# A decoder layer on one Trainium2 core: the forgetting heads' bias loaded as causal strips of the running sums, without the query's own sum

## The chip, the cores and the metric

The kernel runs on one core of a Trainium2 chip. It is one launch that computes a whole decoder layer. The time is device microseconds of that core. Five engines work side by side, each in the order of its own instruction stream: TensorE (PE; its weight loads are listed as PEld), VectorE (DVE), ScalarE (ACT), GpSimd (POOL) and SyncE (SP). Here SP does nothing but issue DMA transfers; they are numbered as work of its queue, SPq. An engine that meets an instruction whose operands are not there yet stands still, and everything behind that instruction in its stream stands still with it.

Times come from whole executions of the kernel (the median of several) and from one more execution that was recorded by the profiler, which has a time of its own.

## The reference: what is computed

One sequence of 512 positions with 1024 features goes through a half-step feed-forward block, a mixer, and a second half-step feed-forward block. The mixer projects the normalised input by one wide matrix to the queries, keys and values of two attention branches of 8 heads each, with gates, and merges the two. This case concerns branch A, the forgetting attention:

```python
def fox_attention(q, k, v, log_f):
    S = q.shape[1]
    cum = jnp.cumsum(log_f, axis=1).transpose(0, 2, 1)
    scale = HEAD_DIM ** -0.5
    for start in range(0, S, Q_BLOCK):                     # Q_BLOCK = 128
        end = start + Q_BLOCK
        logits = einsum('bqhd,bkhd->bhqk', q[:, start:end], k[:, :end]) * scale
        logits = logits + cum[:, :, start:end, None] - cum[:, :, None, :end]
        logits = where(kpos <= qpos, logits, NEG_INF)
        p = softmax(logits, axis=-1)
        outs.append(einsum('bhqk,bkhd->bqhd', p, v[:, :end]))
```

`log_f` is one number per head and position. Its running sum `cum` enters a logit twice: with the query's position t (plus) and with the key's position s (minus). Within one row of a softmax the query's term is the same for all keys. Branch B is a sparse attention: an indexer scores all keys, the top 128 of each query stay, and a bias by distance is added.

## The kernel before

**Tiling.** There are 16 heads in the kernel's loop (`for g in range(2 * H)`): heads 0 to 7 are the forgetting ones, 8 to 15 the sparse ones. Each head has four blocks of 128 queries, worked from the last to the first: step s = 0, 1, 2, 3 is block i = 3, 2, 1, 0. Block i sees n = 128 (i + 1) keys, so its tiles are 128 x 512, 384, 256 and 128.

**One block** is the function `softmax_block`, and goes through all engines:

- the bias of the block is made (`bias(i)`);
- TensorE multiplies queries and keys into one of two PSUM buffers (`stack_mm`, lines 928 and 929). The scores carry the opposite sign, so the softmax works with a minimum in place of a maximum;
- VectorE adds the bias and takes each row's minimum `mn` in one instruction (line 1238);
- ScalarE takes the exponential, with each row's sum `rs` (line 1240);
- VectorE inverts `rs` (line 1241), and POOL multiplies the row by it (line 1242), giving the probabilities `p`.

**Values.** One head later, `flip` transposes the probabilities (TensorE, line 1249). The first of a head's four transposed tiles takes a 128 x 128 piece of all four blocks, so it needs `p` of block 0, the last one made. ScalarE and VectorE split the transposed tile into a rounded part `ph` (1253) and a rest `pl` (1254), and `weigh` multiplies both by the values (lines 1259 and 1260). `head_out` adds up a head's output (POOL in line 1270 for the first heads, VectorE splits it in line 1274).

**What fills TensorE.** Between these small products the loop runs pieces of the large projections (`prod.run`), whose weights SP loads (line 143), ScalarE rounds (144) and VectorE splits (150). Beside the first forgetting head the top-k of the sparse branch still runs on VectorE (lines 1187 to 1192), and the key projections are normalised on POOL (`kn`, line 1002; `rh`, line 900).

**The bias of a forgetting head.** A late piece of the indexer's stage, `forget`, computes the running sums: `cum` holds them with positions on the partitions, `ncum` (line 1174, VectorE) is their negative, and a transposed copy goes to a DRAM array `cum_rows` of 8 rows of 512. For head g, `get_bias(g)` loads row g once, repeated on all 128 partitions (line 1306, one DMA of 256 KB into a tile `cb` of which there are two). For each block, `bias(i)` then takes a scratch tile and has POOL do

```python
G.tensor_scalar(b[:, :n], cb[:, :n], 1.0, ncum[:, i, g:g + 1], op0=OP.mult, op1=OP.add)   # line 1312
G.affine_select(out=b[:, i * P:n], in_=b[:, i * P:n], ..., fill=BIG, ...)                   # line 1313
```

The first adds the query's own sum to the key's, the second writes a large number over the keys behind the query in the last 128 columns. The row of head g + 1 is loaded at step 0 of head g. For the sparse heads the same function loads another bias, and POOL subtracts.

**What sets the order.** TensorE's order is that of the program text. The instructions of VectorE, ScalarE, POOL and SP are put in order by a scheduler before the kernel is built, from its own estimate of when each could run; the order is fixed from then on. A change of some instructions makes the scheduler lay out all four streams anew. A tile name with two buffers lets the second user of a buffer start when all readers of the first are done, and a whole tile is released at once.

## Time and profile before

| | before |
|---|---|
| median of 3 timed runs | 1047.29 us (1047.10 to 1047.31) |
| the profiled execution's own time | 1047.09 us |
| its span | 1045.4 us |
| mean granted TensorE clock | 0.999 |
| TensorE busy | 1033.6 us (99%) |
| VectorE busy | 852.9 us (82%) |
| ScalarE busy | 669.0 us (64%) |
| POOL busy | 259.3 us (25%) |

The span is the time from the first to the last recorded instruction; the execution's own time is 1.7 us longer. A busy share is an average over stages: POOL is busy for 25% of the span, but the page's row of 40 slices shows it at 8 to 9 tenths in one slice and at 1 tenth in many others. A gap is a stretch in which an engine has nothing running; the profile puts in brackets how long it was and which instruction's end ended it. Where line numbers are named without more, they are those of the kernel before; from the change on, those of the functions above lie two lower.

### The profile page before, as it was taken

To read this page: it belongs to the slowest core of one execution; us is meant where nothing else is said; L and a number is where in the kernel's file an instruction comes from. 1 tells how busy PE (TensorE), PEld (TensorE's weight loads), DVE (VectorE), ACT (ScalarE), POOL (GpSimd) and SP (SyncE) were. 2 spreads that over 40 slices of the span, in tenths; PEclk is the share of its full clock that TensorE was granted. 3 is DMA by queue.
4 is the path that set the end of the run, shared out by engine and by line. 5 is a ranking of instruction groups with operands and counts; after the bars stand their busy time and mean duration, and the time that the engine had idled before them with its cause. 6 is when DMAs were issued, how large, how long until landed. Compare 5 with 4: busy or idle time off the path is not lost.

```text
span 1045.4 us, 19485 instructions
## 1 busy us (share of the span) xinstructions
PE 1033.6 (99%) x7424; PEld 962.6 (92%) x7424; DVE 852.9 (82%) x1405; ACT 669.0 (64%) x1118; POOL 259.3 (25%) x324
## 2 busy tenths in 40 slices
PE   9999999999999999999999999999999999999998
PEld 8889999999999898989977788888889999999998
DVE  6897888897989689977778765854887888988887
ACT  6547765865777766567867665433735865775773
POOL 1100111120121024386977653000100210111111
PEclk9999999999999999999999999999999999999999
DMA  7444765666567358633324321532553666567554
GB/s 259 105 151 120 158 165 129 152 163 173 120 150 182 91 147 192 188 104 90 92 69 117 117 70 51 158 131 74 131 168 90 152 147 182 127 160 190 135 127 131
DMA packets 57341, 142.66 MB, mean 136 GB/s; under 512 B 6424, under 2 KB 15768, under 8 KB 57248
## 3 DMA queue, kind: packets, MB, share of 16 engines
q1 hardware_dynamic: 39600, 110.21, 34.7%
q0 software_dynamic: 17504, 30.94, 16.5%
q8 instruction: 58, 0.95, 0.4%
q10 hardware_dynamic: 144, 0.27, 0.1%
q14 instruction: 35, 0.29, 0.1%
HBM read 104.94 MB, written 3.42 MB: 104 GB/s over the span
## 4 chain that ended last, share of the span: by engine, by line
PE 86%; DVE 9%; POOL 2%; issue 2%; ACT 1%; DVEq 0%; POOLq 0%; ACTq 0%
PE pB L157 5%; PE pB L156 5%; PE pB L155 5%; PE pA L157 3%; PE pA L155 3%; PE pA L156 3%; PE ps_f L155 3%; PE ps_f L156 3%; PE ps_f L157 3%; PE dB L157 2%; PE dB L155 2%; PE dB L156 2%; DVE sc L1189 2%; DVE m L1187 2%; PE dA L156 2%
## 5 line engine op out<-in xcount | busy, mean ns | idle before, releaser
L123 ACT CAST wh<-s 128x1024 fp32r<-128x1024 f32 (+1 forms) x90 | 86.7, 963 | 66.1 <-PE pC L156 31.6
L130 DVE TENSOR_TENSOR wl<-s,wh 128x1024 fp32r<-128x1024 f32 (+1 forms) x90 | 100.2, 1113 | 20.0 <-ACT wh L123 20.0
L155 PE MATMUL ps_t<-wh,xh 128*128 128x256 f32 (+1 forms) x288 | 81.1, 282 | 0.0
L156 PE MATMUL ps_t<-wl,xh 128*128 128x256 f32 (+1 forms) x288 | 80.2, 279 | 0.0
L157 PE MATMUL ps_t<-wh,xl 128*128 128x256 f32 (+1 forms) x288 | 80.2, 279 | 0.0
L155 PE MATMUL pB<-tbh,wh 128*128 128x256 f32 x288 | 79.5, 276 | 0.0
L156 PE MATMUL pB<-tbl,wh 128*128 128x256 f32 x288 | 79.5, 276 | 0.0
L157 PE MATMUL pB<-tbh,wl 128*128 128x256 f32 x288 | 79.5, 276 | 0.0
L249 POOL DMA_DIRECT2D b<-gu x12 | 10.4, 864 | 220.4 <-DVE rb L449 89.4
L155 PE MATMUL ps_f<-xh,wh 128*128 128x512 f32 x152 | 60.8, 400 | 0.0
L157 PE MATMUL ps_f<-xh,wl 128*128 128x512 f32 x152 | 59.6, 392 | 0.0
L156 PE MATMUL ps_f<-xl,wh 128*128 128x512 f32 x152 | 59.6, 392 | 0.0
L1240 ACT ACTIVATE p<-p,mn 128x512 f32<-128x512 f32 (+1 forms) x64 | 36.0, 562 | 30.8 <-DVE mn L1238 30.5
L155 PEld LDWEIGHTS ps_t<-wh,xh 128*128 128x128 f32 x288 | 54.4, 189 | 0.4
L156 PEld LDWEIGHTS ps_t<-wl,xh 128*128 128x128 f32 x288 | 54.4, 189 | 0.4
L157 PEld LDWEIGHTS ps_t<-wh,xl 128*128 128x128 f32 x288 | 54.4, 189 | 0.0
L157 PEld LDWEIGHTS pB<-tbh,wl 128*128 128x128 f32 x288 | 54.1, 188 | 0.0
L155 PEld LDWEIGHTS pB<-tbh,wh 128*128 128x128 f32 x288 | 54.1, 188 | 0.0
L156 PEld LDWEIGHTS pB<-tbl,wh 128*128 128x128 f32 x288 | 54.1, 188 | 0.0
L575 POOL DMA_DIRECT2D gx<-e x20 | 23.9, 1241 | 119.6 <-ACT wh L123 99.9
L1242 POOL TENSOR_SCALAR p<-p,rs 128x512 f32<-128x512 f32 (+1 forms) x64 | 39.1, 614 | 57.8 <-DVE rs L1241 53.8
L1254 DVE TENSOR_TENSOR pl<-pt,ph 128x512 fp32r<-128x512 f32 (+1 forms) x64 | 31.0, 484 | 19.6 <-ACT ph L1253 19.4
(406 smaller groups left out, 4195.1 us busy)
## 6 DMA issues: line engine op xcount, KB each, us to landing
rf<-in_w_pair_dram SPq DMA_DIRECT2D x15, 512.0 KB, 4.1
rc<-in_w_pair_dram SPq DMA_DIRECT2D x12, 512.0 KB, 3.6
re<-in_w_pair_dram SPq DMA_DIRECT2D x12, 512.0 KB, 3.6
rd<-in_w_pair_dram SPq DMA_DIRECT2D x12, 512.0 KB, 3.9
rb<-in_w_pair_dram SPq DMA_DIRECT2D x12, 512.0 KB, 4.2
gx<-e POOLq DMA_DIRECT2D x22, 256.0 KB, 4.2
ra<-in_w_pair_dram SPq DMA_DIRECT2D x9, 512.0 KB, 3.5
rd<-in_w_halves_dram SPq DMA_DIRECT2D x12, 384.0 KB, 3.7
```

Source lines behind the costliest of these rows:

```text
L123: S.copy(wh[:, :f], raw[:, :f])
L130: V.tensor_sub(wl[:, :f], raw[:, :f], wh[:, :f].bitcast(F32))
L155: PE.matmul(out, lh, rh, start=start, stop=False, **more)
L156: PE.matmul(out, lh, rl, start=False, stop=False, **more)
L157: PE.matmul(out, ll, rh, start=False, stop=stop, **more)
L249: G.dma_start(l, src, accum_op=OP.add)
L575: G.dma_start(xa[:, d:d + 2, HT:], t["e"][part], accum_op=OP.add)
L1187: V.max(m8, sc[i])
L1189: V.match_replace(out=sc[i], in_to_replace=m8, in_values=sc[i], imm_value=-3e38)
L1240: S.activation(p, p, AF.Exp, bias=mn, scale=-1.0, accum_out=rs)
L1242: G.tensor_scalar(p, p, rs, 1.0, op0=OP.mult, op1=OP.mult)
L1254: V.tensor_sub(pl[:, sl], pt[:, sl], ph[:, sl].bitcast(F32))
```

## The change

A new function `causal_rows(g, i)` makes the bias of one block of a forgetting head. It loads the first n = 128 (i + 1) sums of row g, repeated on 128 partitions, as a strip of its own (line 1309 now), and writes the large number into the strip's last 128 columns in place (line 1310 now). VectorE's addition reads the strip itself. The addition of the query's own sum is left out, and with it `ncum`, its instruction, and the scratch tile of the bias. The softmax's result is the same without it.

So for each forgetting head there are four DMAs (of 128 x 512, 384, 256 and 128 numbers) in place of one, and four selects in place of four additions and four selects. The strips of blocks 3 and 2 take the two buffers that `cb` had. Those of blocks 1 and 0 lie side by side in one tile named `sg`, which an earlier stage used with 4 x (S_W - 128) columns and which is now 384 wide; there is one such tile. The strip of block 3 of head g + 1 is requested at step 0 of head g, that of block 2 at step 1, and those of blocks 1 and 0 at step 3. The sparse heads keep their bias as it was.

```diff
-        sg = at.tile([P, NT, S_W - 128], F32, name="sg")
+        sg = at.tile([P, 3 * P], F32, tag="sg", name="sg")[:, :NT * (S_W - 128)].rearrange("p (t c) -> p t c", t=NT)
...
-        cum = at.tile([P, NT, H], F32, name="cum")
-        ncum = at.tile([P, NT, H], F32, name="ncum")
...
+            cum = small.tile([P, NT, H], F32, tag="cr", bufs=1, name="cum")
             V.tensor_copy(cum, pc[:, :NT * H].rearrange("p (t h) -> p t h", t=NT))
-            V.tensor_scalar(ncum, cum, -1.0, None, op0=OP.mult)
...
+        def causal_rows(g, i):
+            if i:
+                strip = at.tile([P, T] if i > 1 else [P, 3 * P], F32, tag="cb" if i > 1 else "sg",
+                                bufs=2 if i > 1 else 1, name="cb")
+            else:
+                strip = strips[1][:, 2 * P:]
+            n = P * (i + 1)
+            nc.sync.dma_start(strip[:, :n], cum_rows[g:g + 1, :n].to_broadcast([P, n]))
+            G.affine_select(out=strip[:, i * P:n], in_=strip[:, i * P:n], compare_op=OP.is_ge, fill=BIG, base=0,
+                            pattern=[[-1, P]], channel_multiplier=1)
+            strips[i] = strip
+
+        strips = {}
+
+        def forget_bias(i):
+            return strips[i][:, :P * (i + 1)]
+
         def get_bias(g):
             cb = at.tile([P, T], F32, tag="cb", bufs=2, name="cb")
-            nc.sync.dma_start(cb, cum_rows[g:g + 1, :].to_broadcast([P, T]) if g < H else a["rel"][g - H])
+            nc.sync.dma_start(cb, a["rel"][g - H])
 
             def bias(i):
                 n = P * (i + 1)
                 b = tmp_tile("b")
-                if g < H:
-                    G.tensor_scalar(b[:, :n], cb[:, :n], 1.0, ncum[:, i, g:g + 1], op0=OP.mult, op1=OP.add)
-                    G.affine_select(out=b[:, i * P:n], in_=b[:, i * P:n], compare_op=OP.is_ge, fill=BIG, base=0,
-                                    pattern=[[-1, P]], channel_multiplier=1)
-                else:
-                    G.tensor_sub(b[:, :n], sc[i] if i else cpos, cb[:, T - n:T])
+                G.tensor_sub(b[:, :n], sc[i] if i else cpos, cb[:, T - n:T])
                 return b[:, :n]
             return bias
...
             if step == 24:
-                nb = get_bias(0)
+                for i in (3, 2, 1, 0):
+                    causal_rows(0, i)
...
-            q, k, bias = nq, nk, nb
+            q, k, bias = nq, nk, forget_bias if g < H else nb
...
                 if g + 1 < 2 * H:
-                    if s == 0:
+                    if g + 1 < H:
+                        for i in ((3,), (2,), (), (1, 0))[s]:
+                            causal_rows(g + 1, i)
+                    elif s == 0:
                         nb = get_bias(g + 1)
```

TensorE's stream is the same before and after. The other four are laid out anew. Three places show how.

POOL around head 0. Each row is one instruction; `x4` stands for four in a row. Rows with `p` normalise a block (512 wide is block 3, 128 wide block 0); the additions make the biases, the selects mask them. Before, from the last addition and the selects of head 0 on:

```order
L1312 TENSOR_SCALAR b<-cb,ncum 128x128
L1313 AFFINE_SELECT b<-b 128x128 x4
L1242 TENSOR_SCALAR p<-p,rs 128x512
L1312 TENSOR_SCALAR b<-cb,ncum 128x512
L1313 AFFINE_SELECT b<-b 128x128
L1242 TENSOR_SCALAR p<-p,rs 128x384
L1242 TENSOR_SCALAR p<-p,rs 128x256
L1242 TENSOR_SCALAR p<-p,rs 128x128
L1312 TENSOR_SCALAR b<-cb,ncum 128x384
```

The same place now:

```order
L1310 AFFINE_SELECT cb<-cb 128x128 x5
L1240 TENSOR_SCALAR p<-p,rs 128x512
L1310 AFFINE_SELECT cb<-cb 128x128
L1240 TENSOR_SCALAR p<-p,rs 128x384
L1240 TENSOR_SCALAR p<-p,rs 128x256
L1310 AFFINE_SELECT cb<-cb 128x128 x2
L1240 TENSOR_SCALAR p<-p,rs 128x128
L1310 AFFINE_SELECT cb<-cb 128x128
```

The additions are gone. The first five selects are those of head 0 and of block 3 of head 1; the next one is of block 2 of head 1, and the two that follow are those of blocks 1 and 0 of head 1. They stand ahead of the normalisation of head 0's block 0, where before no work for head 1's last two blocks stood. The same order of two selects ahead of block 0's normalisation is found in heads 3 and 5.

VectorE in head 2, around the addition for block 0 (`ps_qk,b 128x128`), the weight split of line 150 and the reciprocals. Before:

```order
L1238 ISA p,mn<-ps_qk,b 128x128
L1238 ISA mn 128x1
L1238 ISA p,mn<-ps_qk,b 128x512
L1238 ISA mn 128x1
L150 TENSOR_TENSOR wl<-rb,wh 128x1024
L1254 TENSOR_TENSOR pl<-pt,ph 128x128
L1241 RECIPROCAL rs<-rs 128x1 x2
```

Now:

```order
L1236 ISA p,mn<-ps_qk,cb 128x128
L1236 ISA mn 128x1
L896 TENSOR_SCALAR ss<-ss 128x8
L1239 RECIPROCAL rs<-rs 128x1
L1236 ISA p,mn<-ps_qk,cb 128x512
L1236 ISA mn 128x1
L150 TENSOR_TENSOR wl<-rb,wh 128x1024
L1252 TENSOR_TENSOR pl<-pt,ph 128x128
L1239 RECIPROCAL rs<-rs 128x1
```

One reciprocal (block 1's) now follows block 0's addition, with a small operation of the key normalisation ahead of it; the last one, block 0's, still follows the weight split.

SP, from the request of head 0's bias on, before:

```order
L1306 DMA cb<-cum_rows 128x512
L143 DMA rc<-in_w_fq_dram 128x1024
L1041 DMA kept<-gs 128x512
L1306 DMA cb<-cum_rows 128x512
L143 DMA ra<-in_w_fq_dram 128x1024
L1306 DMA cb<-cum_rows 128x512
L143 DMA rb<-in_w_fv_dram 128x1024
```

Now:

```order
L1309 DMA cb<-cum_rows 128x512
L1309 DMA cb<-cum_rows 128x384
L1039 DMA kept<-gs 128x512
L1309 DMA cb<-cum_rows 128x256
L1309 DMA cb<-cum_rows 128x128
L143 DMA rc<-in_w_fq_dram 128x1024
L143 DMA ra<-in_w_fq_dram 128x1024
L143 DMA rb<-in_w_fv_dram 128x1024
L1309 DMA cb<-cum_rows 128x512
```

The four strips of head 0 go out ahead of the next weight load, which before stood behind one row.

## The prediction

> **What bounds the kernel now.** I read the page first, then the busy time by stretches, then TensorE's own waits, then the timeline of each gap. From the page:

> ```profile
> span 1045.4 us, 19485 instructions
> PE 1033.6 (99%) x7424; PEld 962.6 (92%) x7424; DVE 852.9 (82%) x1405; ACT 669.0 (64%) x1118; POOL 259.3 (25%) x324
> ```

> TensorE is idle for only 1045.4 - 1033.6 = 11.8 us, and the change leaves TensorE's instructions and their order as they are. So only idle time can be won, and only where the forgetting heads run (432 to 537 us). The stretches of 40, 40 and 20 us there (columns: stretch, length, then busy PE, PEld, DVE, ACT, POOL, the granted clock, the DMA share and GB/s):

> ```profile
> 440.00:480.00 40.00, 36.20 (x291) 34.69 (x289) 31.73 (x83) 27.12 (x61) 31.89 (x44) 1.00 0.34 99
> 480.00:520.00 40.00, 39.60 (x312) 38.08 (x311) 30.81 (x78) 32.25 (x73) 29.12 (x46) 1.00 0.36 95
> 520.00:540.00 20.00, 18.92 (x100) 15.38 (x98) 15.79 (x35) 14.18 (x34) 16.26 (x23) 1.00 0.21 57
> ```

> TensorE is idle here for 3.80 + 0.40 + 1.08 = 5.28 us: the ceiling of any gain, although POOL is 73 to 81% busy. The clock is full and the DMA engines are two thirds empty. One row of TensorE's waits (whole span: total, count, longest), and the larger gaps in its timeline (in brackets, the idle time before the instruction):

> ```profile
> PE pt L1249 <- POOL p L1242: 3.1, 3, 1.5
> ...
> 440.94 0.33 PE L928 MATMUL ps_qk<-kh,st 128*128 128x128 f32 x1 [0.57 <-DVE mn L1238]
> ...
> 448.73 0.33 PE L1249 MATMUL pt<-ident,p 128*128 128x128 f32 x1 [1.48 <-POOL p L1242]
> ...
> 470.07 0.33 PE L928 MATMUL ps_qk<-kh,st 128*128 128x128 f32 x1 [0.34 <-DVE mn L1238]
> ...
> 477.67 0.33 PE L1249 MATMUL pt<-ident,p 128*128 128x128 f32 x1 [1.40 <-POOL p L1242]
> ...
> 524.40 0.39 PE L1260 MATMUL po<-pl,fv 128*128 128x256 f32 x1 [0.75 <-DVE pl L1254]
> ...
> 527.53 0.33 PE L1249 MATMUL pt<-ident,p 128*128 128x128 f32 x1 [0.22 <-POOL p L1242]
> ```

> 3.1 us of the 5.28 is one event in three heads: the flip of a head's probabilities (line 1249) waits for POOL's normalisation (line 1242) of the last block, block 0. I write p(0,0) for head 0, block 0, and DVE(0,0) for VectorE's addition of bias and scores there. The question for each head is when POOL reaches p(g,0).

> **Removed: 32 additions on POOL and one VectorE instruction.** POOL by group, 425 to 540 us (busy, mean ns, idle before):

> ```profile
> L1313 POOL TENSOR_SCALAR_AFFINE_SELECT b<-b 128x128 f32<-128x128 f32 x32 | 9.2, 306 | 0.3
> L1312 POOL TENSOR_SCALAR b<-cb,ncum 128x384 f32<-128x384 f32 x8 | 6.6, 831 | 0.0
> L1312 POOL TENSOR_SCALAR b<-cb,ncum 128x512 f32<-128x512 f32 x8 | 6.6, 821 | 10.1 <-DMA cb<-cum_rows 10.1
> ...
> L1312 POOL TENSOR_SCALAR b<-cb,ncum 128x256 f32<-128x256 f32 x8 | 5.7, 712 | 0.0
> ...
> L1312 POOL TENSOR_SCALAR b<-cb,ncum 128x128 f32<-128x128 f32 x8 | 3.0, 374 | 0.0
> ```

> POOL loses 6.6 + 6.6 + 5.7 + 3.0 = 21.9 us; the 32 selects (9.2 us) stay, now on the strips. Nearly all of it lies beside busy matmuls and is worth nothing. It counts in two places.

> *Head 2 (gaps 0.34 and 1.40 us).* Around its flip, and line 150's group over 334.9 to 690.9 us (least, median, most):

> ```profile
> 469.45 0.56 DVE L1238 CUSTOM_DVE_ANT_0 p<-ps_qk,b 128x384 f32<-128x384 f32 x1 [0.38 <-POOL b L1313]
> 474.53 2.34 DVE L150 TENSOR_TENSOR wl<-rb,wh 128x1024 fp32r<-128x1024 f32 x1
> 477.00 0.20 DVE L1241 RECIPROCAL rs<-rs 128x1 f32<-128x1 f32 x2
> ...
> 474.75 1.04 POOL L1002 TENSOR_TENSOR kn<-kn,rh 128x512 f32<-128x512 f32 x1
> 477.24 1.04 POOL L1242 TENSOR_SCALAR p<-p,rs 128x128 f32<-128x128 f32 x2 [1.45 <-DVE rs L1241]
> ...
> L150 DVE TENSOR_TENSOR wl<-rb,wh x17: 681/1219/2342, 334.9 to 690.9; 128x1024 fp32r<-128x1024 f32 x12, 128x512 fp32r<-128x512 f32 x5
> ```

> The 0.34 is VectorE waiting 0.38 us for a select behind POOL's additions; that goes. The 1.40 is the weight split of line 150, which sits ahead of the reciprocal and took 2.34 us beside POOL's kn, where the median is 1.22. In POOL's new order kn stands before p(2,2), so this meeting should go; then the reciprocal is done 1.1 us earlier, but a 128x8 operation (rh) now sits right ahead of p(2,0), so I count 0.85 of the 1.40. Term: -0.34 - 0.85 = **-1.2**; bounds -1.74 (both gaps) and -0.3 (the split meets another POOL operation and stays long).

> [...]

> *Small gaps of heads 4 to 6 (0.75, 0.22).*

> ```profile
> 521.38 2.56 DVE L1274 TENSOR_TENSOR oAl<-o,oAh 64x512 fp32r<-64x512 f32 x1
> 522.92 1.60 POOL L1312 TENSOR_SCALAR b<-cb,ncum 128x128 f32<-128x128 f32 x2
> ...
> 470.00 0.80 DVE L1274 TENSOR_TENSOR oAl<-o,oAh 64x512 fp32r<-64x512 f32 x1
> ```

> The operation that took 0.80 us elsewhere took 2.56 us beside the additions, and the split of pt behind it is what TensorE waited 0.75 us for. Term: **-0.8** of 0.97, bounds -0.97 and 0.

> **Added and moved: four strips for one row, with the selects on them.** A head's bias is now 128 x (512 + 384 + 256 + 128) x 4 bytes = 640 KB instead of 256 KB, in 4 issues instead of one. With DMA engines 64% free that moves no weight load by itself; without that cover the casts would wait for their weights. The order matters more. Strips 1 and 0 of head g+1 share one buffer with those of head g, so SP can issue them only after DVE(g,0); their selects wait for the landing; and in POOL's new order these two selects stand ahead of p(g,0) in heads 0, 3 and 5 (in head 1 one does). Behind them wait p(g,0), the flip, and so TensorE. Before, p(g,0) waited for its reciprocal alone. What is late next is TensorE itself.

> The price is the landing time L of a small strip. The rows: head 0, the landings (KB, median us from issue to landing), and the cast and split of the first weight that SP now loads behind the four strips.

> ```profile
> 412.48 1.50 DVE L1174 TENSOR_SCALAR ncum<-cum 128x32 f32<-128x32 f32 x1
> ...
> 445.38 0.08 DVE L1238 DVE_READ_ACCUMULATOR2_ANT mn<- 128x1 f32 x1
> ...
> 448.28 0.40 POOL L1242 TENSOR_SCALAR p<-p,rs 128x128 f32<-128x128 f32 x1 [1.57 <-DVE rs L1241]
> ...
> 444.22 0.33 SPq L143 DMA_DIRECT2D ra<-in_w_dq_dram  x1
> ...
> kh<-kh SPq DMA_DIRECT2D x1, 128.0 KB, 2.2
> cb<-cum_rows SPq DMA_DIRECT2D x1, 256.0 KB, 3.0
> cb<-cum_rows SPq DMA_DIRECT2D x3, 256.0 KB, 4.6
> ...
> 432.51 1.05 ACT L144 CAST wh<-rc 128x1024 fp32r<-128x1024 f32 x1 [2.29 <-PE ps_t L157]
> 436.82 1.22 DVE L150 TENSOR_TENSOR wl<-rc,wh 128x1024 fp32r<-128x1024 f32 x1
> ```

> Between the quick 2.2 (128 KB) and 3.0 (256 KB, an issue with no weight load just ahead) I take L = 2.6; behind loads it is 4.6.

> *Head 0.* DVE(0,0) ends at 445.46. The second strip's issue is 0.4 later, then L, the select 0.29, p(0,0) 0.40, 0.05 for signals: 446.6 + L, against TensorE's 448.73, so L - 2.1. The strips go out about 1.3 us behind the 512 KB load of 444.22, for which I add 1.0. The removed `ncum` gives VectorE, full here with the top-k, up to 1.42 us (1.50 less one 0.08 read); I take half, 0.7, since a weight now lies behind the four strips: its cast (432.51) and split (436.82) have 3.3 us between them, which hides the load's delay but not all of it if VectorE comes earlier. So L - 2.1 + 1.0 - 0.7 = L - 1.8 = **+0.8**; bounds -1.1 (the flip waits less by nearly all VectorE gains) and +2.8 (L = 4.6). The 0.57 at 440.94 does not count apart: the flip at 448.73 decides.

> *Heads 3 and 5.* No gap stands before their flips now:

> ```profile
> 485.59 1.22 DVE L150 TENSOR_TENSOR wl<-rc,wh 128x1024 fp32r<-128x1024 f32 x1
> 486.84 0.29 DVE L1238 CUSTOM_DVE_ANT_0 p<-ps_qk,b 128x128 f32<-128x128 f32 x1
> ...
> 490.38 0.38 PE L1249 MATMUL pt<-ident,p 128*128 128x128 f32 x2
> ...
> 510.72 0.09 DVE L1238 DVE_READ_ACCUMULATOR2_ANT mn<- 128x1 f32 x1
> ...
> 513.96 0.27 PE L1249 MATMUL pt<-ident,p 128*128 128x128 f32 x1
> ```

> In the new order DVE(3,0) stands ahead of that split, so it ends at about 485.95. Adding 0.4 + L + 0.69 gives 487.0 + L against 490.38: **0** at 2.6, +1.2 at 4.6. Head 5: 510.81 + 1.1 + L = 511.9 + L against 513.96: **+0.5**, +2.5 at 4.6; 0 when the strip lands in 2.06.

> [...]

> **Sum**, against the profiled execution's own 1047.09: +0.8 - 1.2 + 0 + 0.5 - 0.8 = -0.7, so **1046.4 us**. The median of the timed runs is 1047.29, 0.2 higher, well inside what I can resolve.

> **Rivals.** (1) *The lighter POOL pays in full.* The gaps go except for about a microsecond: strips land early enough (L near 2, head 0 at -1.1), head 2 -1.7, small gaps -1.2 with the unbracketed ones: -4.0, **1043.1**. For it: POOL and VectorE lengthen each other in two quoted rows, and only 3 flips wait for p at all. Against it: new waits stand in three heads. (2) *The late strips hold p(g,0).* POOL, in order, stops at a select whose strip is in the air. With L = 4.6, the row of three: +2.8 + 1.2 + 2.5 - 2.0 = +4.5, **1051.6**. It decides from (L - 1.8) + (L - 3.4) + (L - 2.1) - 2.0 > 2.1, that is L = 3.8. For it: median landings beside weight loads are above that. Against it: the quick rows, and that the strips are a quarter to a half as large. (3) *Nothing is gained.* The time POOL wins is spent waiting for the same reciprocals and row sums, and L is about 3: +1.2 + 0.9 against -1.2 - 0.8, **1047.2**. For it: each p now waits for VectorE's reciprocal (1.57, 1.45 in the rows), not for POOL.

> **How the numbers follow.** Forecast, small terms of both signs: 0.37. Rival 3: 0.13. Rival 1: 0.31. Rival 2: 0.19. 0.2% of 1047 is 2.1 us, about what a measurement here can tell from no change: faster means under 1045.2, slower over 1049.4. The forecast and rival 3 lie within; so faster 0.31, same 0.50, slower 0.19. The range takes in rival 1's 1043.1, and reaches towards rival 2 up to 1050.4 (L about 4.2): about one in ten is left above it, one in ten below.

> **What would show it.** Right: in heads 0 and 5 the flip waits for p, and POOL waits ahead of p(g,0) at a select for a strip's DMA; in head 2 the split of line 150 is near 1.2 us and its gap mostly gone; the 2.56 becomes about 0.8; small strips land in 2.2 to 3.0 us. TensorE's busy time stays at 1033.6. Wrong: no POOL idle time named after a strip's DMA (then rival 1), landings near 4.6 with flip waits of 2 us in heads 0, 3 and 5 (rival 2), or a new gap outside 432 to 540 us, since the schedule was made anew and I priced nothing there.

## The result: slower by 1.2%

The changed kernel takes 1060.06 us (median of 4 runs, 1058.36 to 1060.99), the kernel before 1047.30 us: a ratio of 1.0122, 95% interval 1.0107 to 1.0136. I had forecast 1046.4 us, with a range up to 1050.4.

The first lines of the profile after:

```profile
span 1058.4 us, 19493 instructions
PE 1039.2 (98%) x7424; PEld 968.2 (91%) x7424; DVE 849.5 (80%) x1404; ACT 670.0 (63%) x1118; POOL 240.0 (23%) x292
```

POOL did lose its work (259.3 to 240.0 us busy). The span grew by 13.0 us, in two parts. TensorE is idle for 1058.4 - 1039.2 = 19.2 us in place of 11.8, which is 7.4 more; and it is *busy* for 5.6 us more, with the same 7424 matmuls in the same order. Most of the idle part is in four gaps (TensorE's timeline):

```profile
443.75 0.47 PE L926 MATMUL ps_qk<-kh,st 128*128 128x128 f32 x1 [3.26 <-DVE mn L1236]
...
455.02 0.66 PE L1247 MATMUL pt<-ident,p 128*128 128x128 f32 x4 [2.34 <-POOL p L1240]
...
498.57 0.66 PE L1247 MATMUL pt<-ident,p 128*128 128x128 f32 x4 [1.34 <-POOL p L1240]
...
527.10 0.66 PE L1247 MATMUL pt<-ident,p 128*128 128x128 f32 x4 [3.80 <-POOL p L1240]
```

The last three are flips of heads 0, 3 and 5, where the new order had put two selects ahead of p(g,0). The first is ahead of head 0's scores, where before there were 0.57 us.

The busy part is the granted clock. The windows view, cut at the gaps (stretch, length, busy PE, PEld, DVE, ACT, POOL, clock, DMA share, GB/s):

```profile
440.50:442.75 2.25, 0.00 (x0) 0.00 (x0) 2.25 (x9) 2.24 (x5) 0.00 (x0) 1.00 0.54 127
442.75:449.75 7.00, 6.00 (x26) 5.84 (x27) 6.78 (x22) 4.15 (x11) 3.11 (x5) 0.51 0.37 119
449.75:456.25 6.50, 4.16 (x36) 3.97 (x35) 5.02 (x14) 4.23 (x8) 2.16 (x3) 1.00 0.71 161
456.25:460.00 3.75, 3.75 (x22) 3.75 (x21) 2.69 (x6) 1.71 (x4) 3.39 (x4) 0.54 0.64 199
...
528.00:531.75 3.75, 3.75 (x20) 3.75 (x20) 3.05 (x6) 2.74 (x6) 1.40 (x2) 0.54 0.24 55
```

Each of the three gaps over 2 us is followed by a stretch at about half clock, of 7 or 3.75 us in this view (the first one sets in 1 us before its gap ends); the gap of 1.34 us is followed by none. That loses 6.00 x 0.49 + 2 x 3.75 x 0.46 = 6.4 us of busy time, near the 5.6 more that the page shows.

**Why head 0's scores wait.** SP's issues and the weight's cast and split in the timeline, and its landing (KB, us):

```profile
426.43 0.82 SPq L1309 DMA_DIRECT2D cb<-cum_rows  x2
...
427.79 0.96 SPq L1309 DMA_DIRECT2D cb<-cum_rows  x2
428.85 0.43 SPq L143 DMA_DIRECT2D rc<-in_w_fq_dram  x1
...
438.54 1.05 ACT L144 CAST wh<-rc 128x1024 fp32r<-128x1024 f32 x1 [8.20 <-DMA rc<-in_w_fq_dram]
...
439.62 1.23 DVE L150 TENSOR_TENSOR wl<-rc,wh 128x1024 fp32r<-128x1024 f32 x1 [4.22 <-ACT wh L144]
```

```profile
rc<-in_w_fq_dram SPq DMA_DIRECT2D x1, 512.0 KB, 9.6
```

The weight behind the four strips is cast at 438.54, where it was at 432.51. ScalarE stands still 8.20 us, VectorE 4.22 us, and what is queued behind the split on VectorE, the addition that frees the scores' buffer, comes late.

**Why the flips wait.** POOL in heads 0 and 5, with the issues of the two strips on SP:

```profile
448.30 0.80 SPq L1309 DMA_DIRECT2D cb<-cum_rows  x2
...
452.14 0.29 POOL L1310 TENSOR_SCALAR_AFFINE_SELECT cb<-cb 128x128 f32<-128x128 f32 x1 [2.63 <-DMA cb<-cum_rows]
453.11 0.30 POOL L1310 TENSOR_SCALAR_AFFINE_SELECT cb<-cb 128x128 f32<-128x128 f32 x1 [0.68 <-DMA cb<-cum_rows]
453.38 1.59 POOL L1240 TENSOR_SCALAR p<-p,rs 128x128 f32<-128x128 f32 x1
...
520.95 0.80 SPq L1309 DMA_DIRECT2D cb<-cum_rows  x2
...
524.91 0.29 POOL L1310 TENSOR_SCALAR_AFFINE_SELECT cb<-cb 128x128 f32<-128x128 f32 x1 [4.89 <-DMA cb<-cum_rows]
526.39 0.29 POOL L1310 TENSOR_SCALAR_AFFINE_SELECT cb<-cb 128x128 f32<-128x128 f32 x1 [1.19 <-DMA cb<-cum_rows]
526.67 1.04 POOL L1240 TENSOR_SCALAR p<-p,rs 128x128 f32<-128x128 f32 x2
```

In head 5 POOL waits 4.89 and 1.19 us for the strips of head 6 and only then normalises p(5,0); the flip follows at 527.10. All landings of strips, 425 to 540 us:

```profile
cb<-cum_rows SPq DMA_DIRECT2D x8, 256.0 KB, 3.5
cb<-cum_rows SPq DMA_DIRECT2D x8, 192.0 KB, 3.5
cb<-cum_rows SPq DMA_DIRECT2D x8, 128.0 KB, 3.8
...
cb<-cum_rows SPq DMA_DIRECT2D x8, 64.0 KB, 4.6
```

The smallest strip lands last.

### The profile page after: what moved, and what is told of

It is laid out like the page before. It is cut to its first block, busy times and chain, and to the rows that moved or that the text cites. A ratio compares the mean times of both kernels' runs of the same rounds, so it can differ in the third digit from the quotient of the medians.

```text
span 1058.4 us, 19493 instructions
## 1 busy us (share of the span) xinstructions
PE 1039.2 (98%) x7424; PEld 968.2 (91%) x7424; DVE 849.5 (80%) x1404; ACT 670.0 (63%) x1118; POOL 240.0 (23%) x292
## 4 chain that ended last, share of the span: by engine, by line
PE 91%; DVE 3%; DMA 2%; issue 2%; ACT 1%; POOL 1%; SPq 0%; POOLq 0%; DVEq 0%; ACTq 0%
PE pB L157 5%; PE pB L155 5%; PE pB L156 5%; PE ps_f L155 3%; PE ps_f L157 3%; PE ps_f L156 3%; PE pA L157 3%; PE pA L155 3%; PE pA L156 3%; PE dB L157 2%; PE dB L155 2%; PE dB L156 2%; PE ps_t L155 2%; PE ps_t L157 2%; PE ps_t L156 2%; PE dA L156 2%
## 5 line engine op out<-in xcount | busy, mean ns | idle before, releaser
L155 PE MATMUL ps_t<-wh,xh 128*128 128x256 f32 (+1 forms) x288 | 83.4, 290 | 0.0
L157 PE MATMUL ps_t<-wh,xl 128*128 128x256 f32 (+1 forms) x288 | 82.4, 286 | 0.0
L157 PE MATMUL pB<-tbh,wl 128*128 128x256 f32 x288 | 79.5, 276 | 0.0
L157 PE MATMUL ps_f<-xh,wl 128*128 128x512 f32 x152 | 59.6, 392 | 0.0
L155 PEld LDWEIGHTS ps_t<-wh,xh 128*128 128x128 f32 x288 | 56.9, 198 | 0.5
L156 PEld LDWEIGHTS ps_t<-wl,xh 128*128 128x128 f32 x288 | 56.7, 197 | 0.5
L157 PEld LDWEIGHTS ps_t<-wh,xl 128*128 128x128 f32 x288 | 56.6, 197 | 0.0
L157 PEld LDWEIGHTS pB<-tbh,wl 128*128 128x128 f32 x288 | 54.1, 188 | 0.0
L1238 ACT ACTIVATE p<-p,mn 128x512 f32<-128x512 f32 (+1 forms) x64 | 36.0, 562 | 24.8 <-DVE mn L1236 24.4
## 6 DMA issues: line engine op xcount, KB each, us to landing
gx<-e POOLq DMA_DIRECT2D x22, 256.0 KB, 4.2
```

Of the source, the lines that this page charges most:

```text
L155: PE.matmul(out, lh, rh, start=start, stop=False, **more)
L156: PE.matmul(out, lh, rl, start=False, stop=False, **more)
L157: PE.matmul(out, ll, rh, start=False, stop=stop, **more)
L1238: S.activation(p, p, AF.Exp, bias=mn, scale=-1.0, accum_out=rs)
```

## The experiments

My theory (A): three things add up. A select that waits for a late strip holds p(g,0) on POOL; head 0's strips delay the weight behind them; and a TensorE stall of some length costs clock on top of itself. The rivals: the strips' DMA traffic by itself (B), the late weight alone (C), a worse layout of the streams once the additions are gone (D). Every run is compared with the kernel before on the same chip.

### Selects written where they are used, strips spread, both

In the first run the select moves from the load to the block that reads the strip; in the second head 0's strips are requested at four steps of the loop; the third has both.

```diff
 def forget_bias(i):
-    return strips[i][:, :P * (i + 1)]
+    n = P * (i + 1)
+    G.affine_select(out=strips[i][:, i * P:n], in_=strips[i][:, i * P:n], ...)   # taken out of causal_rows
+    return strips[i][:, :n]
```

```diff
-            if step == 24:
-                for i in (3, 2, 1, 0):
-                    causal_rows(0, i)
+            if step in (24, 26, 28, 29):
+                causal_rows(0, {24: 3, 26: 2, 28: 1, 29: 0}[step])
```

> The changed kernel with one thing moved: a strip is still loaded where it was, but its select is written where the block uses it, so that no select of blocks 1 and 0 of the next head stands ahead of p(g,0). Theory A (a select that waits for a late strip holds p(g,0), and the stall also lowers TensorE's clock): the flip gaps of 2.33, 1.33 and 3.80 us go, with about 2.5 us of lost clock; the gap of 3.26 us ahead of head 0's scores stays, since the strips still lie ahead of the weight. About 1050 us. Rival B (the additional DMA traffic alone slows the stage): still about 1060 us. Rival C (head 0's late weight explains nearly all): above 1055 us.

> The changed kernel with one thing moved: head 0's strips are requested at four steps of the loop in place of one, so that the weight load that was behind four strips is now behind two. Selects stay where they were. Theory A: the weight lands about 3 us earlier, the gap of 3.26 us and the half clock after it (about 3 us) go, the flip gaps of heads 0, 3 and 5 stay: about 1054 us. Rival B (traffic): still 1060. Rival C: about 1049.

> Both of the last two edits. Theory A: both causes gone, TensorE's busy time is back at 1033.6 us, and the lighter POOL pays a little: 1044 to 1047 us. Rival B (traffic, which is the same as in the changed kernel): well above 1050.

Measured: 1058.58 us (ratio 1.0109, 1.0089 to 1.0129), 1057.68 us (1.0105, 1.0088 to 1.0122) and 1056.62 us (1.0094, 1.0079 to 1.0109). All three missed by 3 to 10 us. POOL of the first, in head 5, and TensorE's flip of head 0 in the third:

```profile
521.16 0.29 POOL L1316 TENSOR_SCALAR_AFFINE_SELECT cb<-cb 128x128 f32<-128x128 f32 x1 [4.67 <-DMA cb<-cum_rows]
522.42 0.29 POOL L1316 TENSOR_SCALAR_AFFINE_SELECT cb<-cb 128x128 f32<-128x128 f32 x1 [0.96 <-DMA cb<-cum_rows]
522.69 1.04 POOL L1240 TENSOR_SCALAR p<-p,rs 128x128 f32<-128x128 f32 x2
```

```profile
451.28 1.12 PE L1247 MATMUL pt<-ident,p 128*128 128x128 f32 x4 [5.24 <-POOL p L1240]
```

The first edit did not do what I had written it for: its gaps are still 2.75 us ahead of head 0's scores and 0.56, 1.27 and 3.33 us ahead of the flips of heads 0, 3 and 5. The scheduler took the next head's selects out of their place in the text and set them ahead of p(g,0) again, presumably since in its own estimate the strips are there by then. Spreading the strips did its part: the weight's cast came at 434.89 in the second run and the 3.26 us gap was gone. But then head 0's flip waited longer, 5.10 and 5.24 us: the strip was the next late thing in the same place, and it is late by its own landing, not by the weight. These three runs could not tell A from B.

### One row for a head, masked in place

The blocks are worked from the last to the first, so one row of 512 can serve all four: its last 128 columns are masked for block 3, then the 128 to the left of them for block 2, and so on. One DMA for a head, no additions.

```diff
-            nc.sync.dma_start(strip[:, :n], cum_rows[g:g + 1, :n].to_broadcast([P, n]))    # four strips
+            nc.sync.dma_start(strip, cum_rows[g:g + 1, :].to_broadcast([P, T]))            # one row a head
...
+        def forget_bias(g, i):
+            n = P * (i + 1)
+            strip = rows[g % 2]
+            G.affine_select(out=strip[:, i * P:n], in_=strip[:, i * P:n], ...)
+            return strip[:, :n]
```

> One part of the change alone: no additions and no ncum, but one DMA of 256 KB for a head as in the kernel before; since the blocks are worked from the last to the first, the row is masked in place, 128 columns further left before each block. Theory A (the strips' lateness is the cause, not the lighter POOL or the new order): no flip waits over 2 us, clock full, 1043 to 1047 us. Rival D (taking the additions away lays the streams out badly whatever the loads are): above 1050 us. The in-place select now waits for the block before it to be read; if that is a new wait on TensorE's path, it shows as a gap ahead of the scores.

Measured 1051.19 us (1.0038, 1.0025 to 1.0052). Better by 9 us than the strips, but still with two gaps ahead of flips, 3.90 us in head 0 and 1.77 us in head 5. POOL and SP in head 0:

```profile
443.99 0.33 SPq L1304 DMA_DIRECT2D cb<-cum_rows  x1
...
447.83 1.54 POOL L1312 TENSOR_SCALAR_AFFINE_SELECT cb<-cb 128x128 f32<-128x128 f32 x1 [2.23 <-DMA cb<-cum_rows]
449.35 0.37 POOL L1240 TENSOR_SCALAR p<-p,rs 128x128 f32<-128x128 f32 x1
```

Without any strip the same thing happens: the row that is requested at 443.99, when head 0's last addition frees its buffer, is that of head 2, and its select, a head and a half early, holds p(0,0). So it is the place of the select and not the amount of DMA traffic; that speaks against B.

### The selects tied behind p

The language has an edge for this: `issue_after` keeps an instruction behind a named one on the same engine. The first run below is the changed kernel with that edge alone, the selects where they were. The second has the selects at their use, tied behind p of the head before, and the spread strips. The third is the one row, tied.

```diff
-            G.affine_select(out=strip[:, i * P:n], ...)
+            with tc.issue_after(norm["last"].ins) if norm else nullcontext():      # norm: the p instructions so far
+                G.affine_select(out=strip[:, i * P:n], ...)
```

> The changed kernel with one edge added: each select is issued behind the normalisation that stands before it in the program, so that the selects of head g+1's blocks 1 and 0 come behind p(g,0) on POOL. The first four runs moved the text, yet the order still had a select of a later head ahead of p(0,0) and p(5,0), and their flip gaps stayed. Theory A: the flip gaps of 2.3, 1.3 and 3.8 us shrink to under 1.5 us each; the gap of about 3 us ahead of head 0's scores (the weight behind the strips) and its half clock stay: 1050 to 1053 us. Rival B (DMA traffic or late reciprocals hold p, not the selects): the flip gaps stay, about 1059 us.

> Selects written where the block uses them and issued behind p of the head before (block 3's behind block 2 of the head before), and head 0's strips requested at four steps of the loop, so that the weight is behind two of them. Theory A: no gap over 2 us, TensorE's busy time back at 1033.6 us, 1044 to 1048 us. Rival B (the strips' traffic itself): above 1052 us.

> One row for a head, masked in place, no additions, and the selects issued behind p(g-1,0), or for block 3, whose row comes free only with DVE(g-2,0), behind p(g-2,0). Theory A: the 3.9 and 1.8 us gaps ahead of the flips of heads 0 and 5 go: 1043 to 1047 us, at or below the kernel before. Rival D (the lighter POOL lays the streams out badly in another way): 1050 us as without the edge.

Measured: 1050.07 us (1.0032, 1.0020 to 1.0044), 1045.70 us (0.9987, 0.9978 to 0.9997) and 1043.76 us (0.9968, 0.9956 to 0.9980). All three inside what A expected. In the first, TensorE in head 0 and POOL behind it:

```profile
443.95 0.33 PE L926 MATMUL ps_qk<-kh,st 128*128 128x128 f32 x1 [3.50 <-DVE mn L1236]
...
451.75 0.66 PE L1248 MATMUL pt<-ident,p 128*128 128x128 f32 x4
```

```profile
451.30 0.40 POOL L1240 TENSOR_SCALAR p<-p,rs 128x128 f32<-128x128 f32 x1 [1.35 <-DVE rs L1239]
453.02 1.69 POOL L1312 TENSOR_SCALAR_AFFINE_SELECT cb<-cb 128x128 f32<-128x128 f32 x2 [1.32 <-DMA cb<-cum_rows]
```

This kind of edge alone takes 10 us off. p(0,0) now waits for its reciprocal alone, the selects wait behind it, and the flip has no gap; what stays is the gap ahead of the scores, where the weight is still behind four strips (cast at 438.75) and after which the clock is halved for 3.75 us. With the strips spread as well that goes too. B falls: the second run has the same strips, bytes and packets as the changed kernel and is 14 us faster. D falls too. The third run's first lines:

```profile
span 1043.5 us, 19460 instructions
PE 1033.8 (99%) x7424; PEld 963.0 (92%) x7424; DVE 849.3 (81%) x1404; ACT 668.9 (64%) x1118; POOL 241.4 (23%) x292
```

Busy time is back at 1033.8 us, the clock is full throughout, and the median is 3.4 us under the kernel before. It keeps the idea of the change (no query's sum, no additions). It and the one with eight copies below are the fastest kernels of this study; their intervals overlap. No run has the edges with the additions kept, so how much of the 3.4 us is the lighter POOL's and how much the new order's is not shown.

### The strips alone

The four strips, with the additions and `ncum` of before kept; the select is on the scratch tile again.

```diff
+            b = tmp_tile("b")
+            G.tensor_scalar(b[:, :n], strips[i][:, :n], 1.0, ncum[:, i, g:g + 1], op0=OP.mult, op1=OP.add)
+            G.affine_select(out=b[:, i * P:n], in_=b[:, i * P:n], ...)
```

> The strips alone: four DMAs for a head as in the changed kernel, but POOL keeps the additions (and ncum), from the strip into a scratch tile, and the select on that tile. Theory A: the first weight load again lies behind the strips, so the gap of about 3 us ahead of head 0's scores and one or two stretches of half clock appear (3 + 2 to 3.5); additions that wait for a late strip can hold p(g,0) like the selects did: 1052 to 1060 us. Rival D (what hurts is taking the additions away): 1047 us as before.

Measured 1051.12 us (1.0026, 1.0003 to 1.0049), just under the range. Its cast and its gap ahead of head 0's scores:

```profile
438.45 1.05 ACT L144 CAST wh<-rc 128x1024 fp32r<-128x1024 f32 x1 [8.19 <-DMA rc<-in_w_fq_dram]
```

```profile
443.65 0.47 PE L926 MATMUL ps_qk<-kh,st 128*128 128x128 f32 x1 [3.25 <-DVE mn L1238]
```

The strips alone make the weight late and bring the 3.25 us gap, with 7 us of half clock behind it. Here no addition held p(g,0). So the late weight belongs to the loads; the held flips belong to where the selects were set. C is the first of the two and not nearly all.

### What a stall costs

The kernel before, with idle multiplications by 1.0 put ahead of p(5,0) on POOL, nine of them and three.

```diff
+            if (g, i) == (5, 0):
+                for _ in range(9):          # 3 in the other run
+                    G.tensor_scalar(p, p, 1.0, None, op0=OP.mult)
             G.tensor_scalar(p, p, rs, 1.0, op0=OP.mult, op1=OP.mult)
```

> The kernel before with a known delay: nine idle multiplications by 1.0 of a 128x128 tile on POOL (about 0.37 us each, 3.4 us together) ahead of p(5,0) in head 5 alone. It measures what one stall of TensorE costs. If a stall costs its own length: 1047 + 3.2 = about 1050 us, TensorE busy 1033.6 us. If a stall of over 3 us also lowers the granted clock for some microseconds, as the windows of the changed kernel show: busy 1035 to 1037 us and 1052 to 1054 us.

> The kernel before with three idle multiplications of a 128x128 tile ahead of p(5,0) in place of nine; they took 0.58 us each beside VectorE's work in the run with nine, where TensorE stood still for 8.3 us and then ran at half clock for 5.6 us more. Here the gap should be 1.2 to 1.8 us. If a short stall costs its own length only: busy 1033.6 us and 1048 to 1048.8 us. If any stall costs clock: busy 1035.3 us and about 1050.5 us.

Measured 1056.10 us (1.0085, 1.0069 to 1.0101) with nine and 1052.49 us (1.0040, 1.0018 to 1.0063) with three, both above what I wrote. The nine took 0.53 to 0.60 us each, and the scheduler set three other POOL operations of 0.70, 1.65 and 1.04 us between them, so the stall was 8.27 us; the three stalled TensorE 1.60 us as meant, but the streams laid out anew brought a second gap of 2.73 us later. The long stall, and the clock behind it:

```profile
522.88 1.11 PE L1252 MATMUL pt<-ident,p 128*128 128x128 f32 x4 [8.27 <-POOL p L1245]
```

```profile
518.50:529.00 10.50, 6.12 (x30) 6.12 (x30) 2.47 (x5) 3.08 (x6) 8.88 (x15) 0.51 0.01 2
529.00:535.00 6.00, 6.00 (x35) 5.10 (x33) 4.11 (x12) 4.19 (x11) 1.69 (x4) 1.00 0.29 87
```

and with three:

```profile
514.00:520.00 6.00, 4.40 (x36) 4.25 (x36) 2.17 (x7) 4.84 (x11) 4.84 (x9) 1.00 0.18 46
534.50:538.25 3.75, 3.50 (x10) 2.88 (x11) 3.34 (x10) 2.34 (x6) 1.67 (x3) 0.54 0.48 140
```

A stall alone, in the kernel before, halves the clock: 10.5 us of it here, of which TensorE works 6.1, and busy rises to 1036.0. The 1.60 us stall (514 to 520) leaves the clock full; the one of 2.73 does not. Over all runs, read in steps of a quarter of a microsecond:

| gap ahead of TensorE | runs | half clock that goes with it |
|---|---|---|
| 1.04 to 1.60 us, 15 gaps | before, after and nine others | none |
| 1.77 us | one row, not tied | 3.75 us |
| 2.34 to 3.80 us, 10 gaps | after, selects at use, strips spread, both, tied strips, strips alone, short stall and others | 3.5 to 3.75 us, or 7 us |
| 3.9 to 5.2 us, 3 gaps | one row, spread, both | 3.5 or 7 us |
| 8.27 us | long stall | 10.5 us |

### Why small strips land late

Two edits of the kernel with tied selects and spread strips. In the first the eight rows of sums stand eight times in DRAM, so that 16 partitions share a copy; in the second block 0's strip is requested ahead of block 1's.

```diff
-            nc.sync.dma_start(strip[:, :n], cum_rows[g:g + 1, :n].to_broadcast([P, n]))
+            nc.sync.dma_start(strip[:, :n], cum_rows[:, g:g + 1, :n].to_broadcast([8, 16, n]))
```

```diff
-                        for i in ((3,), (2,), (), (1, 0))[s]:
+                        for i in ((3,), (2,), (), (0, 1))[s]:
```

> The kernel of the sixth run (selects behind p, head 0's strips spread), with the eight rows of sums kept eight times in DRAM, so that 16 partitions read one copy in place of 128. Why does a strip of 64 KB land no sooner (4.3 us) than one of 256 KB (3.4 us)? If all partitions' reads of one row queue at the same address, the strips of 64 and 128 KB land in under 3 us here. If the number of packets or what is ahead in the queue sets it, the landings stay at 3.4 to 4.3 us and the time at 1045 to 1047 us.

> The kernel of the sixth run with the strip of block 0 (64 KB) requested ahead of that of block 1 (128 KB), in place of behind it. In all runs with strips the 64 KB strip landed last: median 4.3 to 5.3 us against 3.4 to 3.9 for the others. If being second in the queue behind 128 packets is what costs, the 64 KB strip now lands in about 3.5 us and the 128 KB strip in 4.3 or more. If a strip's own size or packet size sets it, the 64 KB strip stays at 4.3. The time should stay at 1045 to 1047 us.

Measured 1044.70 us (0.9969, 0.9947 to 0.9990) with copies. The wait for the strips is the same: issued at 444.13 and read by their selects from 448.27 on, against 444.69 and 448.93 without copies. This does not settle it, since the load was also cut in another way (8 x 16 rows in place of 128), SP took about 0.6 us for an issue in place of 0.4, and the weight went ahead of the first strip on SP; the gain of a microsecond is not put down to the copies either. With the small strip first, 1046.06 us (0.9990, 0.9981 to 1.0000), and the landings are

```profile
cb<-cum_rows SPq DMA_DIRECT2D x8, 128.0 KB, 4.6
cb<-cum_rows SPq DMA_DIRECT2D x8, 64.0 KB, 3.8
```

where they were 3.6 us for 128 KB and 4.3 us for 64 KB. Whichever is requested second takes 0.7 to 0.8 us longer from its own request to its landing. A hint at the rest is in the changed kernel's DMA view from 520.0 to 523.5 us, when the two strips of head 6 (issued at 520.95) had the DMA engines to themselves but for the last of it:

```profile
DMA packets 117, 0.11 MB, mean 31 GB/s; under 512 B 8, under 2 KB 117, under 8 KB 117
...
q1 hardware_dynamic: 117, 0.11, 16.6%
```

The first packets move about 1 us after the issue, then 117 of them in 1.5 us, about 13 ns each, while the engines are less than half busy (0.39 of these 1.5 us, 16.6% of the 3.5). A strip is 128 packets whatever its width, one for each partition (the page counts 3072 more packets of 512 B to 2 KB than before, for 24 more transfers); at that pace a pair takes 256 x 13 ns = 3.3 us after the first microsecond. That fits landings that do not fall with the size. But both strips of this pair landed (3.8 and 5.0 us from their requests) about 1.1 us later than this pace gives, and it was not tested by itself, so it stays a reading.

## Why the prediction was wrong, point by point

| | forecast, us | measured, us |
|---|---|---|
| head 0: scores and flip (0.57 and 1.48 became 3.26 and 2.34) | +0.8 | +3.55 |
| head 2 | -1.2 | -1.74 |
| heads 3 and 5: flips | +0.5 | +5.14 |
| small gaps | -0.8 | +0.7 |
| TensorE's busy time | 0 | +5.6 |
| sum (the span grew by 13.0) | -0.7 | +13.2 |

- **What bounds the kernel: right as a place, wrong as a limit.** The flips' wait for p and the heads 0, 3 and 5 were the places. But the idle time was taken for all that could change, and I took the busy time and the clock as given ("TensorE's busy time stays at 1033.6"). It became 1039.2. This step is missing from the sum altogether: 5.6 of the 13.0 us. With gaps of at most 1.48 us, the trace of before could not show it.
- **"That moves no weight load by itself": failed.** The free two thirds of the DMA engines were read from 440 to 520 us. The four strips and the weight load are issued from 426 to 429 us, and there the engines had little free already before; with the strips they are full and move half as much (stretch, length, busy PE, PEld, DVE, ACT, POOL, clock, DMA share, GB/s; before, then after):

```profile
429.00:432.00 3.00, 3.00 (x29) 3.00 (x28) 2.94 (x6) 0.47 (x1) 0.95 (x2) 1.00 0.88 254
429.00:432.00 3.00, 3.00 (x29) 3.00 (x28) 3.00 (x8) 0.48 (x1) 1.02 (x1) 1.00 1.01 128
```

- **Head 0, "which hides the load's delay but not all of it": failed.** I had named the weight behind the strips, but only as a limit on VectorE's gain, and gave it 3.3 us of cover. Its cast came 6.0 us late (issue 2.1 later, landing 9.6 in place of 5.4 us), so the 0.57 us gap that "does not count apart" became 3.26. The strips alone show the same. The flip's own wait grew by only 0.86 us, near the +0.8 of the sum; that is luck, since TensorE itself came late to it.
- **"L = 2.6": mis-sized.** The row that decides is the later of two strips. Their medians are 3.8 and 4.6 us; in head 5 it took 526.39 - 521.35 = 5.0 us from the second issue. I took L from between the quick landings of two single transfers, although the row of three in the same view had 4.6. Sized by 4.6, my own formulas give +1.2 for head 3, where 1.34 was measured, and +2.5 for head 5, where it was 3.80.
- **Head 2, -1.2: right in size, by another way.** Both gaps are gone, -1.74, the bound. Its split of line 150 took 1.22 us in place of 2.34, as forecast. But p(2,0) no longer waits for that split at all:

```profile
479.55 0.16 DVE L1239 RECIPROCAL rs<-rs 128x1 f32<-128x1 f32 x1 [0.48 <-ACT p L1238]
480.80 0.38 POOL L1240 TENSOR_SCALAR p<-p,rs 128x128 f32<-128x128 f32 x1
481.78 1.22 DVE L150 TENSOR_TENSOR wl<-rb,wh 128x1024 fp32r<-128x1024 f32 x1
```

The reciprocal that moved ahead of the split is block 0's, and the one left behind it is that of block 3 of head 3; the section on the change took them for block 1's and block 0's. So the new order removed the 1.40 us gap, and the shorter split would not have been needed; the 0.34 went with the additions, as forecast. POOL's `kn` did not stop meeting splits: another one beside it took 1.99 us (at 474.40), and TensorE did not wait for it.

- **Small gaps, -0.8: half right.** The 0.75 and 0.22 went, and the operation of 2.56 us took 0.68. Gaps of 0.54, 0.49 and 0.62 us in heads 3 to 5 came in their place (TensorE there waits for VectorE), so the term is about +0.7. Such gaps stand in the tied kernels as well, so they belong to the new layout.
- **Rival 2 was the case, at 1051.6 us in place of 1060.** Its mechanism and its places are those of the trace; L = 4.6 was its landing. Its price leaves out the late weight and the clock. I gave it 0.19 because I compared landings; the order of POOL's stream, which I had in hand, was the stronger evidence.
- **Rival 1 has the time of a tied kernel, not its condition.** The one row, tied, takes 1043.76 us, against its 1043.1; but the strips did not land early (3.8 and 4.6 us), the order was changed instead. VectorE's busy time fell by only 3.4 us in the changed kernel.
- **Rival 3 fell for the changed kernel**, which is 12.8 us slower. That the lighter POOL pays once nothing late stands ahead of p is likely from the 3.4 us of the tied kernel, but not shown apart from its new order.

On the loads themselves: tied, one row takes 1043.76 us and the four strips 1045.70, with intervals that just overlap. The forecast gave small strips 2.2 to 3.0 us to land; the medians of the 64 KB strip were 3.8 to 5.3 us in six runs.

## What to carry to other kernels

An instruction that waits for a late transfer also costs what is queued behind it on its engine (in head 5 POOL waited 4.89 and 1.19 us at two selects, and TensorE 3.80 us for the p behind them); when a change lets work for a later stage go early, look at what the order puts behind that work, and tie it behind the urgent instruction if the scheduler's estimate of the transfer is too short. The ordering edge was worth 10 us here, three times the 3.4 us by which the best kernel beats the one before. In a kernel like this one, count a stall of the matrix engine of about 2 us or more as longer than itself: every one of 1.77 us or more had lost clock with it here, 3.50 x 0.46 = 1.6 us with the stall of 2.73 us, 6.00 x 0.49 = 2.9 with that of 3.26, 6.12 x 0.49 = 3.0 with that of 8.27.

## What the runs showed of the hardware that I had not expected

Which of them a gap got was not told by its length (3.26 us: the longer one; 3.80 us: the short one), but by where it lies. In one trace the stretches start whole numbers of 3.413 us apart: those of the changed kernel, at 442.78, 456.44 and 528.12 (6.83, 3.41 and 3.41 us long), are 13.65 and 71.68 us apart, 4 and 21 such windows. Cut into these windows, up to the end of the last matmuls, the traces of all runs agree:

| TensorE idle within one window | windows | the next window |
|---|---|---|
| at full clock, 1.77 to 3.41 us | 15 | half clock |
| at full clock, up to 1.57 us | all others | full clock |
| at half clock, 0.78 to 3.41 us | 7 | half clock |
| at half clock, up to 0.21 us | 15 | full clock |

The changed kernel shows why the shorter gap cost more clock:

| window | TensorE busy, us | granted clock |
|---|---|---|
| 439.37 to 442.78 (gap of 3.26) | 1.12 | 1.00 |
| 442.78 to 446.20 (its end) | 2.45 | 0.50 |
| 446.20 to 449.61 | 3.41 | 0.50 |
| 521.29 to 524.70 (gap of 3.80) | 2.01 | 1.00 |
| 524.70 to 528.12 (its end) | 1.02 | 1.00 |
| 528.12 to 531.53 | 3.41 | 0.50 |

The gap of 3.26 us reached 0.97 us into a half-clock window, and a second one followed. Where the limits lie between 1.57 and 1.77, and between 0.21 and 0.78 us, no run shows. The shortest gap with half clock behind it, 1.77 us in head 5 of the one row, lay within one window.

The 64 KB strip, one DRAM row repeated on 128 partitions, landed no sooner than the 256 KB strip of the same run: 3.8 us where it was requested ahead of the 128 KB one and 4.3 to 5.3 us where behind it, against 3.3 to 3.8 us (medians).
